# First scale and shift by products with c, the spreading of c moved between the transposes of x, half of x scaled before its transposes

## The chip, the cores and the metric

The kernel runs on one core of a Trainium2 chip, without exchange with other cores. The metric is device time in microseconds of the execution, the median of several runs.

## The reference

One decoder layer on x (256 tokens, 1024 channels). What the change touches is its beginning; three token mixers and a gated merge follow and stay as they are:

```python
shift, scale, gate = jnp.split(c @ w_ada[l] + b_ada[l], 3, axis=-1)
h = rmsnorm(x, norm_pre[l]) * (1.0 + scale[:, None]) + shift[:, None]
proj = h @ w_in[l] + b_in[l]
...
x = x + gate[:, None] * rmsnorm(out, norm_post[l])
```

## The kernel before

The large matrix products are made in fp32 by three reduced-precision (fp32r) products: each weight matrix is split by ScalarE (`w_hi`, a cast) and VectorE (`w_lo`, weight minus cast), the activations likewise (`h_hi`, `h_lo`), and TensorE adds hi by hi, lo by hi and hi by lo in PSUM. In this text PE is TensorE, ACT ScalarE, DVE VectorE, SP SyncE.

**Start.** `heat(n)` issues n full fp32 products of ones (a full fp32 product is two passes in the trace). c lies as 8 columns in `p_sb`; eight full products with an identity spread it over all partitions into `ps_cb`, and DVE copies that into `cb`. x (tokens on partitions) is transposed by 16 `flip`s into four PSUM banks `ptr[0..3]`, named `ps_x`; `x_norm` computes the row factors `r`, and two products spread them along the free axis (`ps_rx`, then `rrow`). `evac_x(i)` reads bank i, multiplies it with `rrow` and writes two of the eight 128-channel blocks of `xn`.

**First wave.** A loop over k, the eight channel blocks, with the names of the code: `a_raw` gets the scale and the shift rows of w_ada for block k, `w_raw` 2048 columns of w_in. `ada_dot` multiplies such rows with `cb` and sums along the row on DVE (into `adac`), which gives scale and shift of the block as columns `acol` and `bcol`. ACT makes `h_hi` and `h_f` from `xn`, DVE `h_lo`. PE then does the 48 products of pass k into eight PSUM banks `w0_0` to `w0_7`, all that there are (the trace calls them `w`): first group 0 to 3 with `hi[0]`, `lo[0]`, then 4 to 7 with `hi[1]`, `lo[1]`, in each half 8 hi by hi and 16 others. The next stage begins with `ps_f`.

**What sets the order.** Each engine does its instructions as the code issues them; the helper class Loom (line 174 in the profile stands for all of its instructions, 204 for its loads) keeps modelled times by which later, woven work is placed, and adds no waits. Tiles come from rings: 4 raw buffers, 3 of `hi`, 3 of `lo`, and PSUM banks of three kinds, `BANKS = dict(mm=3, sd=3, ml=2)`. A new tile in a used buffer waits for the last reader of the old tile. `ptr` takes kinds mm, sd, ml, ml; `ps_cb` two of sd; `w0_0` to `w0_2` are mm, `w0_3` to `w0_5` sd, `w0_6` and `w0_7` ml.

Of the kernel before, what the change touches and what calls it, by code (L numbers as in the profile page):

```python
# [60 lines left out]
CATCH = 7  # L61
BRANCHES = ((2, "c"), (0, "a"), (1, "b"))
AHEAD = {2: ((0, 1), ()), 0: ((0,), (1,)), 1: ((0, 1), ())}
HEAT = (5, 3, 6)
# [212 lines left out]
def trunk(ctx: ExitStack, tc, xtok, wada, wave0, wgrp, wmisc, w1, wbr, wout, par, vbias, out):  # L277
# [26 lines left out]
    def bank(name, kind="mm"):  # L304
        return loom.alloc(psum.tile([128, 512], F32, name=name, tag=kind, bufs=BANKS[kind]), kind, BANKS[kind])
# [39 lines left out]
    ps_cb = [bank("ps_cb", "sd") for _ in range(2)]  # L345
    for i in range(2):
        for j in range(4):
            mm(ps_cb[i][:, 128 * j:128 * j + 128], pc("c", 4 * i + j).broadcast_to([128, 128]), ident, True, True)
        dve.tensor_copy(cb[:, 512 * i:512 * i + 512], ps_cb[i])
        drop(ps_cb[i])  # L350
# [122 lines left out]

    for t in range(2):
        act.activation(xnf[:, D * t:D * t + D], x_sb[:, t], AF.Square, accum_out=ss[:, t:t + 1])
        for k in range(KT):
            flip(ptr[k // 2][:, 256 * (k % 2) + 128 * t:256 * (k % 2) + 128 * t + 128],
                 x_sb[:, t, 128 * k:128 * k + 128])
    act.activation(r, ss, AF.Sqrt, bias=eps, scale=1.0 / D)
    heat(HEAT[1])  # L480

    def x_norm():
# [22 lines left out]
    banks = [bank(f"w0_{f}", kinds[f]) for f in range(8)]  # L505
    for k in range(KT):
        raw = rawt([128, 2, D], "a_raw")
        wraw = rawt([128, 2, 1024], "w_raw")
        for i in range(2):
            loom.load(nc.sync, raw[:, i], wada[k, :, i])  # L510
        for i in range(2):
            loom.load(nc.sync, wraw[:, i], wave0[k, :, 1024 * i:1024 * i + 1024])
        if k == 0:
            dve.tensor_scalar(v, ss, 1.0 / D, 1e-6, op0=OP.mult, op1=OP.add)
        ada_dot(raw[:, 0], 8 + k)
        if k == 0:
            x_norm()
        ada_dot(raw[:, 1], k)
        if k == 0:
            evac_x(0)  # L520
        a, b = acol[:, k:k + 1], bcol[:, k:k + 1]
        dve.scalar_tensor_tensor(a, adac[:, 8 + k:9 + k], 1.0, pc("b_ada", 8 + k), op0=OP.add, op1=OP.add)
        dve.tensor_tensor(b, adac[:, k:k + 1], pc("b_ada", k), op=OP.add)
        dve.tensor_tensor(a, a, pc("npre", k), op=OP.mult)
# [3 lines left out]
        act.copy(hi[0], wraw[:, 0])  # L528
        if 4 < k < CATCH:
            act.copy(hi[1], wraw[:, 1])  # L530
        if k == 0:
            heat(HEAT[2])
        act.activation(h_hi[:, k], xn[:, k], AF.Identity, scale=a, bias=b)
        act.activation(h, xn[:, k], AF.Identity, scale=a, bias=b)
        if k < 5 or k >= CATCH:
            act.copy(hi[1], wraw[:, 1])
        if k == KT - 3:
            act.activation(warm, warm, AF.Sigmoid)
        dve.tensor_tensor(lo[0], wraw[:, 0], hi[0], op=OP.subtract)
# [953 lines left out]
```

## Time and profile before

| | us |
|---|---|
| median of 3 runs (lowest, highest) | 506.78 (506.33, 507.31) |
| the profiled execution's own time | 506.12 |
| its span, first to last instruction | 504.4 |
| PE busy | 492.6 |
| DVE busy | 433.6 |
| ACT busy | 306.5 |

The span lies inside the execution's time; 1.7 us are around it. An engine's busy time tells how near it is to being the bound; what a change is worth is read from the stage that it touches.

### The profile page before, as it was taken

Reading aid. Unit: us, or ns where it says so; the run is one execution under the profiler, and the core shown is the slowest. Engines: PE = TensorE matmul, PEld = TensorE weight load, DVE = VectorE, ACT = ScalarE, POOL = GpSimd, SP = SyncE. Lnnn points to the kernel's source line nnn. Section 1 sums busy time; section 2 is a strip of 40 time slices with the busy share of each in tenths; the row PEclk is TensorE's granted clock in tenths of the full one; section 3 lists DMA queues with packets and bytes.
Section 4 is the critical chain, followed back from the end, with each engine's and each line's share of the span. In section 5 each row is a group of like instructions: output and inputs, shape, how many; then the busy total and the mean of one; then the engine's idle time right before and its main releaser. Section 6 shows DMA issues by size and latency. Waiting matters only on the chain.

```text
span 504.4 us, 8492 instructions
## 1 busy us (share of the span) xinstructions
PE 492.6 (98%) x3229; PEld 437.5 (87%) x3229; DVE 433.6 (86%) x872; ACT 306.5 (61%) x518; POOL 7.3 (1%) x41
## 2 busy tenths in 40 slices
PE   7999999999999999999999999999999999999994
PEld 7999999789878989978899799997888788888883
DVE  3999889999999999999799899669998986756755
ACT  3647665335464759979587874666666835354442
POOL 5000000000000000000000000000000000000000
PEclk9999999999999999999999999999999999999998
DMA  8999964874776243414235236455277586655402
GB/s 308 343 357 340 417 265 176 325 279 164 266 303 252 92 159 97 165 73 168 84 136 199 84 120 251 175 182 210 109 294 299 204 343 233 259 203 209 168 0 83
DMA packets 18200, 105.85 MB, mean 210 GB/s; under 512 B 2152, under 2 KB 2288, under 8 KB 8048
## 3 DMA queue, kind: packets, MB, share of 16 engines
q1 hardware_dynamic: 18016, 105.29, 55.9%
q8 instruction: 25, 0.41, 0.3%
q14 instruction: 15, 0.12, 0.1%
q10 hardware_dynamic: 144, 0.03, 0.0%
HBM read 104.26 MB, written 1.05 MB: 209 GB/s over the span
## 4 chain that ended last, share of the span: by engine, by line
PE 90%; DVE 6%; ACT 2%; issue 1%; DMA 1%; DVEq 0%; ACTq 0%
PE ps_f L174 37%; PE ps_t L174 30%; PE w L174 5%; PE ps_out L174 4%; PE ps_o L174 3%; PE ps_s L174 2%; DVE w_lo L174 2%; DVE a_raw L174 2%; PE ps_c L174 2%; PE ps_p L174 1%; PE ps_qk L174 1%; PE ps_n L174 1%; DMA p_sb<-in_par_dram 1%; ACT w_hi L174 1%; PE ps_cb L174 1%
## 5 line engine op out<-in xcount | busy, mean ns | idle before, releaser
L174 DVE TENSOR_TENSOR w_lo<-w_raw,w_hi 128x1024 fp32r<-128x1024 f32 x148 | 179.8, 1219 | 38.5 <-ACT w_hi L174 37.1
L174 ACT CAST w_hi<-w_raw 128x1024 fp32r<-128x1024 f32 x148 | 154.6, 1045 | 74.7 <-PE ps_t L174 52.4
L174 PE MATMUL ps_f<-h_hi,w_hi 128*128 128x256 f32 x512 | 130.0, 290 | 0.0
L174 PE MATMUL ps_f<-h_lo,w_hi 128*128 128x256 f32 x512 | 126.2, 283 | 0.0
L174 PEld LDWEIGHTS ps_f<-h_hi,w_hi 128*128 128x128 f32 x512 | 98.0, 191 | 1.9 <-issue 1.1
L174 PEld LDWEIGHTS ps_f<-h_lo,w_hi 128*128 128x128 f32 x512 | 98.1, 192 | 0.6 <-issue 0.2
L174 DVE SCALAR_TENSOR_TENSOR acc<-u,p_sb,acc 128x226 f32<-128x226 f32 (+28 forms) x232 | 93.0, 459 | 2.0 <-ACT acc L174 1.9
L174 PE MATMUL ps_f<-h_hi,w_lo 128*128 128x256 f32 x512 | 75.8, 288 | 0.0
L174 PEld LDWEIGHTS ps_f<-h_hi,w_lo 128*128 128x128 f32 x512 | 66.9, 191 | 3.0 <-issue 1.8
L174 PE MATMUL ps_t<-w_hi,h_hi 128*128 128x512 f32 x144 | 57.4, 398 | 0.2 <-DVE gs L174 0.2
L174 PE MATMUL ps_t<-w_hi,h_lo 128*128 128x512 f32 x144 | 56.2, 391 | 0.0
L174 PE MATMUL ps_t<-w_lo,h_hi 128*128 128x512 f32 x144 | 44.9, 393 | 0.0
L174 PEld LDWEIGHTS ps_t<-w_hi,h_hi 128*128 128x128 f32 x144 | 27.1, 188 | 6.8 <-issue 0.8
L174 PEld LDWEIGHTS ps_t<-w_lo,h_hi 128*128 128x128 f32 x144 | 27.0, 188 | 5.7
L174 ACT ACT_TABLE_LOAD x24 | 30.8, 1283 | 1.6 <-PEq L1485 1.2
L174 PEld LDWEIGHTS ps_t<-w_hi,h_lo 128*128 128x128 f32 x144 | 27.1, 188 | 5.3
L174 PE MATMUL w<-h_lo,w_hi 128*128 128x256 f32 x128 | 31.4, 283 | 0.0
L174 PE MATMUL w<-h_hi,w_lo 128*128 128x256 f32 x128 | 31.3, 282 | 0.0
L174 DVE SCALAR_TENSOR_TENSOR a_raw<-a_raw,cb 128x1024 f32<-128x1024 f32 x24 | 28.6, 1218 | 0.0
L174 PEld LDWEIGHTS w<-h_hi,w_lo 128*128 128x128 f32 x128 | 24.5, 191 | 0.0
L174 PEld LDWEIGHTS w<-h_lo,w_hi 128*128 128x128 f32 x128 | 24.5, 191 | 0.0
L174 ACT ACTIVATE pm<-pm,mx 128x16 f32<-128x16 f32 (+2 forms) x48 | 19.0, 401 | 1.9 <-DVE mx L174 1.9
(261 smaller groups left out, 697.7 us busy)
## 6 DMA issues: line engine op xcount, KB each, us to landing
w_raw<-in_wgrp_dram SPq DMA_DIRECT2D x50, 1024.0 KB, 4.9
w_raw<-in_wbr_dram SPq DMA_DIRECT2D x12, 1024.0 KB, 4.8
a_raw<-in_wada_dram SPq DMA_DIRECT2D x16, 512.0 KB, 6.8
w_raw<-in_wave_dram SPq DMA_DIRECT2D x16, 512.0 KB, 6.5
w_raw<-in_w_dram SPq DMA_DIRECT2D x8, 1024.0 KB, 4.8
a_raw<-in_wada_dram SPq DMA_DIRECT2D x4, 1024.0 KB, 4.8
w_raw<-in_wout_dram SPq DMA_DIRECT2D x4, 1024.0 KB, 4.7
vb_mg<-in_vbias_dram SPq DMA_DIRECT2D x3, 512.0 KB, 5.7
```

What stands on the lines that cost most here:

```text
L174: inst = self.pin(fn(*args, **kw))
```

## The change

Scale and shift of block 0 no longer come from `ada_dot`: w_ada's first pair is laid out untransposed, and 16 full products (8 for scale, 8 for shift) with 128x128 pieces of it as stationary operand and c, repeated over 32 columns, as moving operand leave them as columns in PSUM (`ps_a`). The eight products that spread c move between the transposes of x, four behind each half's first four transposes; DVE copies the first half of `cb`, ACT the second, later. Channels 512 to 1023 of x are scaled by `r` in place before they are transposed, so that ACT's evacuation of `ptr[2]` and `ptr[3]` needs only a factor, and two later products with `rrow` on DVE go. The first two `w_raw` come in three loads. In passes 0 and 1 DVE makes `h_hi`, the cast of `hi[0]` goes in two halves, and in pass 0 `lo[0]` does too. Block 1's scale product moves ahead of the last split of pass 0; `evac_x(1)` moves from pass 0 to the end of pass 1. The heats are 8 and 1, before 5, 3 and 6.

```diff
--- before.py
+++ after.py
@@ -59,9 +59,10 @@
 NEARLY = 56
 
 CATCH = 7
+NREP = 32
 BRANCHES = ((2, "c"), (0, "a"), (1, "b"))
-HEAT = (5, 3, 6)
+HEAT = (8, 1)
 LEAD = 2
 BANKS = dict(mm=3, sd=3, ml=2)
@@ -342,12 +343,6 @@
     ident = const.tile([128, 128], F32, name="ident")
     make_identity(nc, ident)
     cb = const.tile([128, D], F32, name="cb")
-    ps_cb = [bank("ps_cb", "sd") for _ in range(2)]
-    for i in range(2):
-        for j in range(4):
-            mm(ps_cb[i][:, 128 * j:128 * j + 128], pc("c", 4 * i + j).broadcast_to([128, 128]), ident, True, True)
-        dve.tensor_copy(cb[:, 512 * i:512 * i + 512], ps_cb[i])
-        drop(ps_cb[i])
@@ -471,13 +466,18 @@
                           rrow[:, None, :].broadcast_to([128, 2, S]), op=OP.mult)
         drop(ptr[i])
 
+    ps_cb = [bank("ps_cb", "sd") for _ in range(2)]
+
+    def flip_x(k, t):
+        flip(ptr[k // 2][:, 256 * (k % 2) + 128 * t:256 * (k % 2) + 128 * t + 128], x_sb[:, t, 128 * k:128 * k + 128])
+
     for t in range(2):
         act.activation(xnf[:, D * t:D * t + D], x_sb[:, t], AF.Square, accum_out=ss[:, t:t + 1])
-        for k in range(KT):
-            flip(ptr[k // 2][:, 256 * (k % 2) + 128 * t:256 * (k % 2) + 128 * t + 128],
-                 x_sb[:, t, 128 * k:128 * k + 128])
+        for k in range(KT // 2):
+            flip_x(k, t)
+        for j in range(4):
+            mm(ps_cb[t][:, 128 * j:128 * j + 128], pc("c", 4 * t + j).broadcast_to([128, 128]), ident, True, True)
     act.activation(r, ss, AF.Sqrt, bias=eps, scale=1.0 / D)
-    heat(HEAT[1])
 
     def x_norm():
         dve.reciprocal(r, r)
@@ -487,6 +487,9 @@
         ps = bank("ps_rx")
         for t in range(2):
             mm(ps[:, 128 * t:128 * t + 128], r[:, t:t + 1].broadcast_to([128, 128]), ident, True, True)
+        late = [x_sb[:, t, D // 2:] for t in range(2)]
+        dve.tensor_scalar(late[0], late[0], r[:, 0:1], None, op0=OP.mult)
+        act.mul(late[1], late[1], r[:, 1:2])
         act.mul(rrow, ps[:, 0:S], -0.5)
         drop(ps)
 
@@ -502,52 +505,87 @@
     bcol = const.tile([128, 8], F32, name="bcol")
 
     kinds = [k for k in BANKS for _ in range(BANKS[k])]
-    banks = [bank(f"w0_{f}", kinds[f]) for f in range(8)]
+    raws_, wraws = [], []
     for k in range(KT):
-        raw = rawt([128, 2, D], "a_raw")
-        wraw = rawt([128, 2, 1024], "w_raw")
-        for i in range(2):
-            loom.load(nc.sync, raw[:, i], wada[k, :, i])
-        for i in range(2):
-            loom.load(nc.sync, wraw[:, i], wave0[k, :, 1024 * i:1024 * i + 1024])
-        if k == 0:
-            dve.tensor_scalar(v, ss, 1.0 / D, 1e-6, op0=OP.mult, op1=OP.add)
-        ada_dot(raw[:, 0], 8 + k)
-        if k == 0:
-            x_norm()
-        ada_dot(raw[:, 1], k)
-        if k == 0:
-            evac_x(0)
-        a, b = acol[:, k:k + 1], bcol[:, k:k + 1]
-        dve.scalar_tensor_tensor(a, adac[:, 8 + k:9 + k], 1.0, pc("b_ada", 8 + k), op0=OP.add, op1=OP.add)
-        dve.tensor_tensor(b, adac[:, k:k + 1], pc("b_ada", k), op=OP.add)
-        dve.tensor_tensor(a, a, pc("npre", k), op=OP.mult)
+        for j in range(k, k + 2 if k == 0 else k + 1 if k > 1 else k):
+            raw = rawt([128, 2, D], "a_raw")
+            wraw = rawt([128, 2, 1024], "w_raw")
+            raws_.append(raw)
+            wraws.append(wraw)
+            for i in range(2):
+                loom.load(nc.sync, raw[:, i], wada[j, :, i])
+            cuts = (0, 512, 1024, 2048) if j < 2 else (0, 1024, 2048)
+            flat = wraw.rearrange("p a b -> p (a b)")
+            for c0, c1 in zip(cuts, cuts[1:]):
+                loom.load(nc.sync, flat[:, c0:c1], wave0[j, :, c0:c1])
+        raw, wraw = raws_[k], wraws[k]
         hi = [ringt(his, [128, 1024], "w_hi", "hi", HIS, F32R) for _ in range(2)]
         lo = [ringt(los, [128, 1024], "w_lo", "lo", LOS, F32R) for _ in range(2)]
         h = h_f[:, k]
-        act.copy(hi[0], wraw[:, 0])
-        if 4 < k < CATCH:
-            act.copy(hi[1], wraw[:, 1])
+        a, b = acol[:, k:k + 1], bcol[:, k:k + 1]
         if k == 0:
-            heat(HEAT[2])
-        act.activation(h_hi[:, k], xn[:, k], AF.Identity, scale=a, bias=b)
+            dve.tensor_copy(cb[:, 0:512], ps_cb[0])
+            drop(ps_cb[0])
+            dve.tensor_scalar(v, ss, 1.0 / D, 1e-6, op0=OP.mult, op1=OP.add)
+            ps_a = [bank("ps_a", kind) for kind in ("mm", "sd")]
+            for i in range(2):
+                for j in range(KT):
+                    mm(ps_a[i][:, 0:NREP], raw[:, i, 128 * j:128 * j + 128], pc("c", j).broadcast_to([128, NREP]),
+                       j == 0, j == KT - 1)
+                if i == 0:
+                    x_norm()
+                    evac_x(0)
+            mods = [p[:, 0:1] for p in ps_a]
+        else:
+            if k > 1:
+                ada_dot(raw[:, 0], 8 + k)
+            ada_dot(raw[:, 1], k)
+            mods = adac[:, 8 + k:9 + k], adac[:, k:k + 1]
+        dve.scalar_tensor_tensor(a, mods[0], 1.0, pc("b_ada", 8 + k), op0=OP.add, op1=OP.add)
+        dve.tensor_tensor(a, a, pc("npre", k), op=OP.mult)
+        dve.tensor_tensor(b, mods[1], pc("b_ada", k), op=OP.add)
+        if k == 0:
+            drop(*ps_a)
+            for t in range(2):
+                for j in range(KT // 2, KT):
+                    flip_x(j, t)
+            heat(HEAT[1])
+        if k < 2:
+            act.copy(hi[0][:, 0:512], wraw[:, 0, 0:512])
+            dve.tensor_scalar(h_hi[:, k], xn[:, k], a, b, op0=OP.mult, op1=OP.add)
+            act.copy(hi[0][:, 512:], wraw[:, 0, 512:])
+        else:
+            act.copy(hi[0], wraw[:, 0])
+            if 4 < k < CATCH:
+                act.copy(hi[1], wraw[:, 1])
+            act.activation(h_hi[:, k], xn[:, k], AF.Identity, scale=a, bias=b)
         act.activation(h, xn[:, k], AF.Identity, scale=a, bias=b)
+        if k == 0:
+            act.copy(cb[:, 512:], ps_cb[1])
+            drop(ps_cb[1])
         if k < 5 or k >= CATCH:
             act.copy(hi[1], wraw[:, 1])
         if k == KT - 3:
             act.activation(warm, warm, AF.Sigmoid)
-        dve.tensor_tensor(lo[0], wraw[:, 0], hi[0], op=OP.subtract)
-        dve.tensor_tensor(h_lo[:, k], h, h_hi[:, k], op=OP.subtract)
         if k == 0:
+            dve.tensor_tensor(lo[0][:, 0:512], wraw[:, 0, 0:512], hi[0][:, 0:512], op=OP.subtract)
+            dve.tensor_tensor(h_lo[:, k], h, h_hi[:, k], op=OP.subtract)
+            dve.tensor_tensor(lo[0][:, 512:], wraw[:, 0, 512:], hi[0][:, 512:], op=OP.subtract)
+            for i in range(2, 4):
+                act.mul(xn[:, 2 * i:2 * i + 2], ptr[i].rearrange("p (k s) -> p k s", k=2), -0.5)
+                drop(ptr[i])
+        else:
+            dve.tensor_tensor(lo[0], wraw[:, 0], hi[0], op=OP.subtract)
+            dve.tensor_tensor(h_lo[:, k], h, h_hi[:, k], op=OP.subtract)
+        if k == 0:
+            ada_dot(raws_[1][:, 0], 9)
+        dve.tensor_tensor(lo[1], wraw[:, 1], hi[1], op=OP.subtract)
+        if k == 1:
             evac_x(1)
-            for i in range(2, 4):
-                act.copy(xn[:, 2 * i:2 * i + 2], ptr[i].rearrange("p (k s) -> p k s", k=2))
-                drop(ptr[i])
-        dve.tensor_tensor(lo[1], wraw[:, 1], hi[1], op=OP.subtract)
-        if k in (3, 5):
-            c = xn[:, k + 1:k + 3]
-            dve.tensor_tensor(c, c, rrow[:, None, :].broadcast_to([128, 2, S]), op=OP.mult)
         drop(raw, wraw)
+
+        if k == 0:
+            banks = [bank(f"w0_{f}", kinds[f]) for f in range(8)]
 
         def w0(f, j, w, x, start, stop):
             c = (f % 4) * 256 + j * 128
...
+    pairs[0] = np.stack([ktiles(wa[i, 0].T) for i in (1, 0)], 1)
```

How the change moves instructions, at three places. The names are those of the tiles with their buffer numbers; a bracket names the engine or DMA queue whose counter the instruction waits for, and a wait for a counter covers all earlier work of that engine.

PE at the program's start, before (`ps_x_157` to `ps_x_160` are `ptr[0]` to `ptr[3]`):

```order
L174 MATMUL ps_heat_94<-ones_84 128x128 [waits Pool_49]
L174 MATMUL ps_heat_94<-ones_84 128x128 x4
L174 MATMUL ps_cb_107<-ident_101,p_sb_90 128x128 [waits DMAHW0_49,Pool_49]
L174 MATMUL ps_cb_107<-ident_101,p_sb_90 128x128 x3
L174 MATMUL ps_cb_108<-ident_101,p_sb_90 128x128 x4
L174 MATMUL ps_x_157<-ident_101,x_sb_89 128x128 [waits DMAHW1_49]
L174 MATMUL ps_x_157<-ident_101,x_sb_89 128x128
L174 MATMUL ps_x_158<-ident_101,x_sb_89 128x128 x2
L174 MATMUL ps_x_159<-ident_101,x_sb_89 128x128 x2
```

And in the change (`ps_x_148` and `ps_x_149` are `ptr[0]` and `ptr[1]`):

```order
L175 MATMUL ps_heat_94<-ones_84 128x128 [waits Pool_49]
L175 MATMUL ps_heat_94<-ones_84 128x128 x7
L175 MATMUL ps_x_148<-ident_104,x_sb_89 128x128 [waits DMAHW1_49,Pool_49]
L175 MATMUL ps_x_148<-ident_104,x_sb_89 128x128
L175 MATMUL ps_x_149<-ident_104,x_sb_89 128x128 x2
L175 MATMUL ps_cb_156<-ident_104,p_sb_90 128x128 [waits DMAHW0_49]
L175 MATMUL ps_cb_156<-ident_104,p_sb_90 128x128 x3
L175 MATMUL ps_x_148<-ident_104,x_sb_89 128x128 [waits DMAHW2_49]
L175 MATMUL ps_x_148<-ident_104,x_sb_89 128x128
L175 MATMUL ps_x_149<-ident_104,x_sb_89 128x128 x2
L175 MATMUL ps_cb_157<-ident_104,p_sb_90 128x128 x4
L175 MATMUL ps_a_203<-p_sb_90,a_raw_183 128x32 [waits DMAHW3_49]
```

The products with c stood ahead of all transposes and now stand behind four of each half; the transposes of `ptr[2]` and `ptr[3]` have moved behind the products `ps_a`.

PE in pass 0, from the end of the first half (groups 0 to 3) into the second, before:

```order
L174 MATMUL w0_3_197<-h_hi_189,w_lo_225 128x256
L174 MATMUL w0_4_198<-h_hi_189,w_hi_224 128x256 [waits Activation_49]
L174 MATMUL w0_4_198<-h_hi_189,w_hi_224 128x256
L174 MATMUL w0_5_199<-h_hi_189,w_hi_224 128x256 [waits DVE_49]
L174 MATMUL w0_5_199<-h_hi_189,w_hi_224 128x256
L174 MATMUL w0_6_200<-h_hi_189,w_hi_224 128x256 [waits Activation_49]
L174 MATMUL w0_6_200<-h_hi_189,w_hi_224 128x256
L174 MATMUL w0_7_201<-h_hi_189,w_hi_224 128x256 [waits Activation_49]
L174 MATMUL w0_7_201<-h_hi_189,w_hi_224 128x256
L174 MATMUL w0_4_198<-h_lo_190,w_hi_224 128x256
L174 MATMUL w0_4_198<-h_hi_189,w_lo_226 128x256 [waits DVE_49]
```

In the change, the same stretch:

```order
L175 MATMUL w0_3_261<-h_hi_178,w_lo_199 128x256
L175 MATMUL w0_4_262<-h_hi_178,w_hi_198 128x256 [waits Activation_49]
L175 MATMUL w0_4_262<-h_hi_178,w_hi_198 128x256
L175 MATMUL w0_5_263<-h_hi_178,w_hi_198 128x256 [waits DVE_49]
L175 MATMUL w0_5_263<-h_hi_178,w_hi_198 128x256
L175 MATMUL w0_6_264<-h_hi_178,w_hi_198 128x256 [waits Activation_49]
L175 MATMUL w0_6_264<-h_hi_178,w_hi_198 128x256
L175 MATMUL w0_7_265<-h_hi_178,w_hi_198 128x256 [waits Activation_49]
L175 MATMUL w0_7_265<-h_hi_178,w_hi_198 128x256
L175 MATMUL w0_4_262<-h_lo_179,w_hi_198 128x256
L175 MATMUL w0_4_262<-h_hi_178,w_lo_200 128x256
```

And the beginning of pass 1 in the change (`w_hi_314`, `w_lo_316` and `h_lo` of block 1):

```order
L175 MATMUL w0_0_258<-h_hi_178,w_hi_314 128x256 [waits Activation_49]
L175 MATMUL w0_0_258<-h_hi_178,w_hi_314 128x256
L175 MATMUL w0_1_259<-h_hi_178,w_hi_314 128x256 x2
L175 MATMUL w0_2_260<-h_hi_178,w_hi_314 128x256 [waits Activation_49]
L175 MATMUL w0_2_260<-h_hi_178,w_hi_314 128x256
L175 MATMUL w0_3_261<-h_hi_178,w_hi_314 128x256 x2
L175 MATMUL w0_0_258<-h_lo_179,w_hi_314 128x256
L175 MATMUL w0_0_258<-h_hi_178,w_lo_316 128x256
```

The first product of group `w0_5` waits for DVE in both. Before, DVE is waited for again for `w_lo_226`, the second split of pass 0; in the change neither `w_lo_200` nor pass 1's `h_lo` and `w_lo_316` has a wait for DVE of its own.

DVE from pass 0's splits on, before (`xn` from `ps_x_158` is `evac_x(1)`; `w_lo_305` and `w_lo_306` are pass 1's):

```order
L174 TENSOR_TENSOR w_lo_225<-w_raw_203,w_hi_223 128x1024 [waits DMAHW5_49,Activation_49]
L174 TENSOR_TENSOR h_lo_190<-h_f_191,h_hi_189 128x256 [waits Activation_49]
L174 TENSOR_TENSOR xn_156<-ps_x_158,rrow_164 128x512 [waits PE_49]
L174 TENSOR_TENSOR w_lo_226<-w_raw_203,w_hi_224 128x1024 [waits DMAHW6_49,Activation_49]
L174 SCALAR_TENSOR_TENSOR a_raw_292,adac_188<-a_raw_292,cb_106 128x1024 [waits DMAHW7_49]
L174 SCALAR_TENSOR_TENSOR a_raw_292,adac_188<-a_raw_292,cb_106 128x1024 [waits DMAHW0_49]
L174 SCALAR_TENSOR_TENSOR acol_192<-adac_188,p_sb_90 128x1 [waits DVE_49]
L174 TENSOR_TENSOR bcol_193<-adac_188,p_sb_90 128x1 [waits DVE_49]
L174 TENSOR_TENSOR acol_192<-acol_192,p_sb_90 128x1 [waits DVE_49]
L174 TENSOR_TENSOR w_lo_305<-w_raw_293,w_hi_303 128x1024 [waits DMAHW1_49,Activation_49]
L174 TENSOR_TENSOR h_lo_190<-h_f_191,h_hi_189 128x256 [waits Activation_49]
L174 TENSOR_TENSOR w_lo_306<-w_raw_293,w_hi_304 128x1024 [waits DMAHW2_49,PE_49,Activation_49]
```

In the change, from the second half of `lo[0]` to `evac_x(1)`, which is `xn` from `ps_x_149`:

```order
L175 TENSOR_TENSOR w_lo_199<-w_raw_184,w_hi_197 128x512 [waits DMAHW6_49]
L175 SCALAR_TENSOR_TENSOR a_raw_190,adac_177<-a_raw_190,cb_109 128x1024 [waits DMAHW0_49,Activation_49]
L175 TENSOR_TENSOR w_lo_200<-w_raw_184,w_hi_198 128x1024 [waits DMAHW7_49,Activation_49]
L175 SCALAR_TENSOR_TENSOR a_raw_190,adac_177<-a_raw_190,cb_109 128x1024 [waits DMAHW1_49]
L175 SCALAR_TENSOR_TENSOR acol_181<-adac_177,p_sb_90 128x1 [waits DVE_49]
L175 TENSOR_TENSOR acol_181<-acol_181,p_sb_90 128x1 [waits DVE_49]
L175 TENSOR_TENSOR bcol_182<-adac_177,p_sb_90 128x1
L175 TENSOR_SCALAR h_hi_178<-xn_147,acol_181,bcol_182 128x256 [waits DVE_49]
L175 TENSOR_TENSOR w_lo_316<-w_raw_191,w_hi_314 128x1024 [waits DMAHW3_49,DMAHW2_49,Activation_49]
L175 TENSOR_TENSOR h_lo_179<-h_f_180,h_hi_178 128x256 [waits DVE_49,Activation_49]
L175 TENSOR_TENSOR w_lo_317<-w_raw_191,w_hi_315 128x1024 [waits DMAHW4_49,PE_49,Activation_49]
L175 TENSOR_TENSOR xn_147<-ps_x_149,rrow_155 128x512
```

`evac_x(1)` stood third and ahead of pass 0's second split; now all DVE work of pass 1 stands ahead of it.

## Rows read from the trace of the kernel before

**Rows 1.** The page: busy time, share and instructions of each engine.

```profile
PE 492.6 (98%) x3229; PEld 437.5 (87%) x3229; DVE 433.6 (86%) x872; ACT 306.5 (61%) x518; POOL 7.3 (1%) x41
```

**Rows 2.** Whom PE waited for, whole span: us in total, times, longest.

```profile
PE w L174 <- ACT h_hi L174: 1.2, 2, 0.8
...
PE ps_t L174 <- DVE w_lo L174: 0.3, 1, 0.3
```

**Rows 3.** PE's timeline to 15 us: start, us; x counts passes; [idle before <-releaser].

```profile
1.05 2.50 PE L174 MATMUL ps_heat<-ones 128*128 128x128 f32 x10 [1.05 <-POOL eps L322]
5.35 3.75 PE L174 MATMUL ps_cb<-ident,p_sb 128*128 128x128 f32 x16 [1.79 <-DMA p_sb<-in_par_dram]
8.89 2.33 PE L174 MATMUL ps_x<-ident,x_sb 128*128 128x128 f32 x16
11.06 0.83 PE L174 MATMUL ps_heat<-ones 128*128 128x128 f32 x6
11.91 0.68 PE L174 MATMUL ps_rx<-ident,xr 128*128 128x128 f32 x4
12.43 1.50 PE L174 MATMUL ps_heat<-ones 128*128 128x128 f32 x12
14.68 1.22 PE L174 MATMUL w<-h_hi,w_hi 128*128 128x256 f32 x8 [0.75 <-ACT h_hi L174]
```

**Rows 4.** PE's timeline in the first wave, and at its end.

```profile
17.65 1.12 PE L174 MATMUL w<-h_hi,w_hi 128*128 128x256 f32 x8
...
56.42 1.12 PE L174 MATMUL w<-h_hi,w_hi 128*128 128x256 f32 x8
...
62.18 0.28 PE L174 MATMUL ps_f<-h_hi,w_hi 128*128 128x256 f32 x1
```

**Rows 5.** DVE's timeline, 11 to 20 us.

```profile
11.01 0.16 DVE L174 RECIPROCAL xr<-xr 128x2 f32<-128x2 f32 x1
...
13.04 0.69 DVE L174 TENSOR_TENSOR xn<-ps_x,rrow 128x512 f32<-128x512 f32 x1
...
15.15 0.42 DVE L174 TENSOR_TENSOR h_lo<-h_f,h_hi 128x256 fp32r<-128x256 f32 x1
15.50 0.68 DVE L174 TENSOR_TENSOR xn<-ps_x,rrow 128x512 f32<-128x512 f32 x1
16.10 1.22 DVE L174 TENSOR_TENSOR w_lo<-w_raw,w_hi 128x1024 fp32r<-128x1024 f32 x1
17.24 1.22 DVE L174 SCALAR_TENSOR_TENSOR a_raw<-a_raw,cb 128x1024 f32<-128x1024 f32 x1
...
19.53 0.15 DVE L174 SCALAR_TENSOR_TENSOR acol<-adac,p_sb 128x1 f32<-128x1 f32 x1
...
19.80 1.22 DVE L174 TENSOR_TENSOR w_lo<-w_raw,w_hi 128x1024 fp32r<-128x1024 f32 x1
```

**Rows 6.** ScalarE's (ACT's) timeline to 13 us.

```profile
5.06 1.06 ACT L174 ACTIVATE xn<-x_sb 128x1024 f32<-128x1024 f32 x1 [2.32 <-DMA x_sb<-in_xtok_dram]
...
12.63 0.38 ACT L174 ACTIVATE rrow<-ps_rx 128x256 f32<-128x256 f32 x1 [4.76 <-PE ps_rx L174]
```

**Rows 7.** PE's timeline at 110 us.

```profile
109.72 0.53 PE L174 MATMUL ps_c<-gather,part 128*128 128x32 f32 x4
110.08 0.36 PE L174 MATMUL ps_f<-h_hi,w_hi 128*128 128x256 f32 x1
```

**Rows 8.** DMA issues from 3 to 6 us: x count, size, median us to landing.

```profile
a_raw<-in_wada_dram SPq DMA_DIRECT2D x2, 512.0 KB, 9.3
```

**Rows 9.** SyncE's timeline from 4 us: its issues.

```profile
4.04 1.51 SPq L204 DMA_DIRECT2D a_raw<-in_wada_dram  x2
```

**Rows 10.** Stretches at the end: length, busy time (x), PEclk, DMA share, GB/s.

```profile
496.00:498.00 2.00, 1.29 (x6) 0.75 (x4) 1.82 (x4) 0.65 (x3) 0.00 (x0) 1.00 0.31 120
498.00:501.00 3.00, 0.00 (x0) 0.00 (x0) 2.72 (x7) 0.28 (x2) 0.00 (x0) 1.00 0.25 95
501.00:502.00 1.00, 0.00 (x0) 0.00 (x0) 0.00 (x0) 0.00 (x0) 0.00 (x0) 0.64 0.88 332
```

## The prediction

> **What bounds the kernel now.** First the page's line of busy shares [rows 1]: TensorE (PE) is busy for 492.6 of 504.4 us, so a microsecond counts only where it starts PE earlier, stops it, or slows it. Then PE's list of waits [rows 2]: after its start it waits 1.2 us for `h_hi` (before the first wave and before one of its later passes) and, as the next longest, 0.3 us once much later. Nothing behind the first wave is slack that could give a late start back. Then PE in order of time [rows 3, 4]: the wave, which is all that the change touches, begins at 14.68 and ends where `ps_f` begins, at 62.18. Its last pass runs from 56.42 to 62.18, 5.76 us for 48 products, 0.12 each, without a wait; eight such passes are 46.1 us and the wave takes 47.5, so its own waits cost 1.4.
>
> **The order, and the place that decides.** The wave needs all eight PSUM banks. Product group `w0_5` gets the bank of `ps_x` number 1 (kind "sd", of which there are three), and may write there only when `evac_x(1)` has read it. Before, that read stands ahead of the wave's first pass on VectorE (DVE): it starts at 15.50 [rows 5], and PE comes to `w0_5` at about 17.9 [rows 4], so the handover costs nothing. In the changed kernel the read comes behind the last split of pass 1. The order shows what PE then waits for: its DVE wait at `w0_5` in pass 0 is the last for a long while, and not even pass 1's first uses of `w_lo` and `h_lo` wait for DVE, so the wait at `w0_5` already covers DVE work of pass 1. PE does 26 products of pass 0, then stops until DVE has done nearly all of pass 1. That wait has no cover: the other 22 products of pass 0 stand behind it on PE's queue, and everything else behind those.
>
> **When DVE gets there.** I follow the new order with the durations of the old rows.
> PE: eight heats keep it at work from 1.05 to about 4.7; x's first half has landed by 5.06 and c by 5.35 [rows 3, 6]. Four transposes and four products with c at the slow pace take 0.9 and 1.7 us. The pace: `ps_cb` took 3.54 us for 16 passes, 0.22 each; the last heats 0.125 each at most. The 16 transposes from 8.89 to 11.06 are 2.17 us, some 4 at the slow pace and 12 at half of it, so the clock rose at about 9.7, when PE had worked for 4.35 us on end. Those are the two levels, 1.2 and 2.4 GHz. With more heats and 0.3 us of idle time in place of 1.8 I take the rise near 6.3; it may be 9.7 again.
> With the rise at 6.3: products with c done at 7.0, transposes of x's other half 7.45, c again 8.35. Sixteen narrow products (32 columns) are new; the nearest rows [rows 7], 32 columns too and two passes to a product, give 0.36 us for two up to the start of the next work, so at most 0.18 each; I take 1.3 us for eight. The first eight end at 9.65. `ps_rx` follows (r is ready by then: half of `cb` copied in 0.7, as `xn` in [rows 5], then 0.9 from the reciprocal to `ps_rx`). From its start to `rrow` 0.72 and to `xn` 1.13 [rows 3, 5, 6]: `xn` starts at 10.8 and ends at 11.4, as the second eight do. a, b and `h_hi` on DVE (like `h_lo`, 0.35) end at 12.15; the wave starts at 12.5 (eight transposes and a heat behind the second eight) in place of 14.68. That is the gain of the change's first part: 2.2 us.
> DVE then does half a split, `h_lo`, half a split (0.6 + 0.35 + 0.6), and at 13.7 the first row product of pass 1, whose data land at 13.3 (issued at 4.04, 9.3 us under way) [rows 8, 9].
> From there to the end of `evac_x(1)`, all from starts of [rows 5]: row product 1.15, split 1.14, row product 1.15, a and b 0.35, `h_hi` 0.35, split 1.14, `h_lo` 0.35, split 1.14, `evac_x(1)` 0.68: 7.45 us. PE goes on at 21.2. Not before 20.75 (data at 13.3 and no other delay); 22.8 if the clock rises only at 9.7, since then every PE step ahead of `h_hi` is later and the row product starts at 15.35.
>
> **The sum.** At 21.2 there remain 22 products (2.6) and seven passes of 5.76 (40.3), now without the 1.4 us of waits, as DVE and ScalarE are ahead: the wave ends at 64.1, 1.9 later than 62.18 (bounds 1.5 and 3.5).
> To that comes the clock. PE stands still from 15.6 to 21.2, 5.6 us. At the end of the program its last product ended at 497.3 (PE is busy for 1.29 of the stretch from 496), and the granted clock was 1.00 up to 501 and 0.64 on average in the next microsecond [rows 10], as full speed up to 501.3 and half from there would give: it fell after 4.0 us without work. So I expect PE to be at 1.2 GHz when it goes on, and to stay there for about the 4.35 us that it took at the start; at half pace that loses 2.1. Bounds: nothing (it doesn't fall), and 3.2, if it takes as long as all the slow work at the start, heats from 1.05 included (2.3 + 4.35).
> The Trainium skill, page "TensorE: Matmul & The Clock Gate", section "HAM oscillation — how this bites in real kernels", says of bursts with long waits between them that each begins at half clock again. The end of this trace agrees for the fall; a fall in mid-program this trace does not have. By the rule the sum has the 2.1, without it not.
> What else the change does lies in the shadow of that stop: two more issues on SyncE, long ahead of need, 1.2 us of `rrow` products taken from DVE in passes 3 and 5, two half-x scalings, one copy of `cb` on ScalarE. Later work is woven in another order; PE's products are the same, and its longest wait there is the 0.3 [rows 2], so I give that 0.5 either way.
> The sum is +4.0 us. The profiled execution took 506.12, so 510.1; the median of the runs is 506.78, 0.66 above it, so the median should come out at **510.8**.
>
> **Rivals.**
> Late clock (0.15): as above, but the rise at 9.7. For it: the trace has a single rise, and it is at 9.7. Against: PE's heats now reach to x's landing. Then +3.5 + 2.1: 512.4.
> No fall (0.13): the stop is there, the clock stays at 2.4 GHz. For it: the only fall seen is at a program's end. Against: 5.6 us is more than the 4.0 there. Then +1.9: 508.7.
> Faster (0.07): DVE's read of `ps_x` number 1 does not hold PE, because what PE waits for at `w0_5` is an earlier DVE step. Then the wave runs from 12.5 for 46.1 us and ends at 58.6, 3.6 earlier: 503.2. It decides from a resume before 19.3 (62.18 less 42.9), or 17.2 if the clock falls. Against: the chain of 7.45 us can't begin before its data at 13.3, and pass 1 has no DVE waits of its own.
> Nothing changes (0.05): a stop that the earlier start just pays for, a resume at 19.3 and no fall.
> The forecast has the remaining 0.60, on its own 509.6 to 511.8. A measurement of this kernel tells about 0.2%, 1.0 us, from no change: slower 0.88, same 0.05, faster 0.07. The range goes from below no fall (508.7 less 0.4 for the early bound of the resume) to the late clock with some of the longer warm-up: 508.2 to 513.2.
>
> **What would show it.** In the changed profile: PE's `w` with a gap of 5 to 6 us between `w0_4` and `w0_5` of pass 0, ended by DVE's `xn`; before it a wave start near 12.5; slices with a granted clock below 1 at about 20 to 26 us; no `h_hi` waits in the wave afterwards; `ps_f` starting near 66. `ps_cb` followed by transposes at the fast pace shows the early rise. Wrong would be: no gap at `w0_5` (the faster rival), products of `w` at 0.12 us right after the gap (no fall), or a gap that lasts beyond 23 (DVE held by something that I have not seen, such as ScalarE's split of pass 1).

## The result, and the profile after

The changed kernel took **511.0 us** in the median of four runs (510.19 to 512.47), the kernel before 506.68: ratio **1.0092** (95% interval 1.0078 to 1.0105), slower by 0.9%. Four more runs, in the experiments, gave 511.77 against 506.12: 1.0107 (1.0093 to 1.0121). The profiled execution is the slowest of the first four, 512.47 (span 510.7). Line 175 is now the helper's line (174 before, 176 in e5 and e8 below).

The page, busy time of each engine (answers to [rows 1]). PE is busy for 5.4 us more with 22 passes more (3251 in place of 3229, at some 0.12 each 2.6 us): the rest is time at a slower pace.

```profile
PE 498.0 (97%) x3251; PEld 443.6 (87%) x3251; DVE 431.7 (85%) x869; ACT 306.2 (60%) x520; POOL 7.3 (1%) x41
```

Whom PE waited for (answers to [rows 2]): the `h_hi` waits of 1.2 us are gone, and one wait of 2.9 us for DVE's `xn` has come.

```profile
PE w L175 <- DVE xn L175: 2.9, 1, 2.9
PE ps_heat L175 <- POOL eps L323: 1.1, 1, 1.1
PE ps_c L175 <- DMA w_raw<-in_w_dram: 0.6, 1, 0.6
```

PE's timeline to 15 us, then around the stop, then the wave's end (answers to [rows 3, 4]).

```profile
1.05 3.55 PE L175 MATMUL ps_heat<-ones 128*128 128x128 f32 x16 [1.05 <-POOL eps L323]
...
7.73 1.92 PE L175 MATMUL ps_a<-p_sb,a_raw 128*128 128x32 f32 x16
9.48 0.69 PE L175 MATMUL ps_rx<-ident,xr 128*128 128x128 f32 x4
10.01 2.50 PE L175 MATMUL ps_a<-p_sb,a_raw 128*128 128x32 f32 x16
12.32 1.95 PE L175 MATMUL ps_x<-ident,x_sb 128*128 128x128 f32 x8
14.06 0.63 PE L175 MATMUL ps_heat<-ones 128*128 128x128 f32 x2
14.34 2.05 PE L175 MATMUL w<-h_hi,w_hi 128*128 128x256 f32 x8
...
18.85 0.40 PE L175 MATMUL w<-h_hi,w_hi 128*128 128x256 f32 x2
22.15 1.65 PE L175 MATMUL w<-h_hi,w_hi 128*128 128x256 f32 x6 [2.90 <-DVE xn L175]
23.60 0.41 PE L175 MATMUL w<-h_lo,w_hi 128*128 128x256 f32 x1
23.81 0.41 PE L175 MATMUL w<-h_hi,w_lo 128*128 128x256 f32 x1
...
62.06 1.12 PE L175 MATMUL w<-h_hi,w_hi 128*128 128x256 f32 x8
64.94 1.12 PE L175 MATMUL w<-h_hi,w_hi 128*128 128x256 f32 x8
67.82 0.28 PE L175 MATMUL ps_f<-h_hi,w_hi 128*128 128x256 f32 x1
```

The wave starts at 14.34 in place of 14.68 and ends at 67.82 in place of 62.18. After two products of `w0_4` PE stops until 22.15, and behind the stop products start 0.21 apart (23.60, 23.81), where the last pass shows 0.12 (5.76 for 48). From the start of `ps_f` to the end of the span are 442.2 us before (504.4 less 62.18) and 442.9 now (510.7 less 67.82), so all but 0.7 us of the loss lies ahead of `ps_f`. A product is listed with 0.28 us though the next one starts 0.12 later, so a delay of less than about 0.16 us counts as busy time and not as idle time.

DVE ahead of `h_hi`, where it waits for the second eight narrow products (`ps_a`), then from the first row product of pass 1 to the read that PE waits for (answers to [rows 5]): 14.61 to 22.10, without a wait.

```profile
12.54 0.16 DVE L175 TENSOR_TENSOR bcol<-ps_a,p_sb 128x1 f32<-128x1 f32 x1 [0.97 <-PE ps_a L175]
...
14.61 1.22 DVE L175 SCALAR_TENSOR_TENSOR a_raw<-a_raw,cb 128x1024 f32<-128x1024 f32 x1
...
20.28 1.22 DVE L175 TENSOR_TENSOR w_lo<-w_raw,w_hi 128x1024 fp32r<-128x1024 f32 x1
21.42 0.68 DVE L175 TENSOR_TENSOR xn<-ps_x,rrow 128x512 f32<-128x512 f32 x1
```

Stretches of 2 us: length, busy time (number) of PE, its weight loads, DVE, ACT and POOL, then the granted clock PEclk, DMA share, GB/s.

```profile
10.00:12.00 2.00, 2.00 (x17) 2.00 (x15) 0.91 (x3) 1.41 (x3) 0.00 (x0) 0.77 1.03 414
12.00:14.00 2.00, 2.00 (x11) 2.00 (x11) 1.42 (x4) 1.26 (x3) 0.00 (x0) 0.50 1.01 408
...
18.00:20.00 2.00, 1.25 (x11) 1.05 (x9) 1.93 (x8) 1.52 (x2) 0.00 (x0) 1.00 1.04 373
20.00:22.00 2.00, 0.00 (x0) 0.00 (x0) 2.00 (x4) 0.02 (x1) 0.00 (x0) 0.83 1.00 350
22.00:24.00 2.00, 1.85 (x8) 1.85 (x9) 2.00 (x4) 0.00 (x0) 0.00 (x0) 0.50 0.97 311
...
28.00:30.00 2.00, 2.00 (x18) 2.00 (x17) 1.56 (x2) 1.12 (x3) 0.00 (x0) 0.97 1.02 418
```

PE was at half clock, 1.2 GHz, in two stretches: one from the stop to about 28 us, as forecast, and one that was not, in 11 to 18 us, where PE was busy without a break. This earlier one hardly counts: it delays the start of a wave that then stands still for DVE anyway. Below, e5 has it and e8 has not, and their waves end at 65.01 and 64.98.

### The profile page after: what moved, and what is told of

It reads as the page before. It is cut to its first block, busy times and chain, and to the rows that moved or that the text cites. A ratio compares the mean times of both kernels' runs of the same rounds, so it can differ in the third digit from the quotient of the medians.

```text
span 510.7 us, 8544 instructions
## 1 busy us (share of the span) xinstructions
PE 498.0 (97%) x3251; PEld 443.6 (87%) x3251; DVE 431.7 (85%) x869; ACT 306.2 (60%) x520; POOL 7.3 (1%) x41
## 4 chain that ended last, share of the span: by engine, by line
PE 89%; DVE 6%; DMA 2%; issue 1%; ACT 0%; DVEq 0%; ACTq 0%
PE ps_f L175 34%; PE ps_t L175 29%; PE w L175 9%; PE ps_out L175 4%; PE ps_o L175 3%; DVE w_lo L175 2%; PE ps_s L175 2%; PE ps_c L175 2%; PE ps_p L175 1%; DMA w_raw<-in_w_dram 1%; PE ps_qk L175 1%; PE ps_n L175 1%; DMA x_sb<-in_xtok_dram 1%; PE ps_a L175 1%; DVE acc L175 1%
## 5 line engine op out<-in xcount | busy, mean ns | idle before, releaser
L175 DVE TENSOR_TENSOR w_lo<-w_raw,w_hi 128x1024 fp32r<-128x1024 f32 (+1 forms) x149 | 180.0, 1212 | 44.7 <-ACT w_hi L175 43.1
L175 ACT CAST w_hi<-w_raw 128x1024 fp32r<-128x1024 f32 (+1 forms) x150 | 154.8, 1034 | 87.3 <-PE ps_t L175 56.5
L175 PE MATMUL ps_f<-h_hi,w_lo 128*128 128x256 f32 x512 | 76.9, 289 | 0.0
L175 PE MATMUL w<-h_lo,w_hi 128*128 128x256 f32 x128 | 33.5, 295 | 0.0
L175 PE MATMUL w<-h_hi,w_lo 128*128 128x256 f32 x128 | 33.4, 295 | 0.0
L175 PEld LDWEIGHTS w<-h_lo,w_hi 128*128 128x128 f32 x128 | 26.3, 206 | 0.0
L175 PEld LDWEIGHTS w<-h_hi,w_lo 128*128 128x128 f32 x128 | 26.2, 205 | 0.0
L175 DVE SCALAR_TENSOR_TENSOR a_raw<-a_raw,cb 128x1024 f32<-128x1024 f32 x22 | 26.2, 1217 | 0.0
L175 PE MATMUL w<-h_hi,w_hi 128*128 128x256 f32 x128 | 20.3, 305 | 2.9 <-DVE xn L175 2.9
```

What stands on the lines that cost most here:

```text
L175: inst = self.pin(fn(*args, **kw))
```

## The experiments

The theory: the late read `evac_x(1)` stops PE at `w0_5`, the standing still makes the clock fall, and these two are the whole loss; the rest of the change is a gain. Rivals: the stop alone costs, and the clock's fall is not paid for; the new 32-column products and their clock cost; the order of later work costs. From `w0_5` on, the wave needs 22 x 0.12 + 7 x 5.76 = 42.96 us at full pace without waits, so in the table "excess" is `ps_f` less the resume less 42.96: what half pace, and waits, took behind the stop. Times in us; each ratio is against the kernel before, timed on the same chip with it (506.36 for e1 to e5, 506.12 for e6 to e9, 506.38 for e10 and e12). A median is of all runs of a kernel; wave, stop and `ps_f` are of its one profiled run.

| kernel | wave starts | stop | resumes | `ps_f` | excess | median | ratio (95%) |
|---|---|---|---|---|---|---|---|
| changed, first profile | 14.34 | 2.90 | 22.15 | 67.82 | 2.71 | 511.0 | 1.0092 (1.0078, 1.0105) |
| e6 changed, again | 13.72 | 5.41 | 22.49 | 67.79 | 2.34 | 511.77 | 1.0107 (1.0093, 1.0121) |
| e7 128 columns | 13.12 | 5.45 | 21.92 | 66.43 | 1.55 | 511.38 | 1.0100 (1.0086, 1.0114) |
| e8 128 columns, stop filled | 13.13 | 0.53, filled | 21.92 | 64.98 | 0.10 | 509.63 | 1.0069 (1.0055, 1.0082) |
| e5 as changed, stop filled in part | 14.14 | 1.56, part filled | 21.95 | 65.01 | 0.10 | 510.11 | 1.0078 (1.0061, 1.0094) |
| e12 read in mid pass 1, 128 | 13.18 | 2.06 | 18.59 | 63.14 | 1.59 | 507.19 | 1.0015 (1.0006, 1.0024) |
| e9 read at end of pass 0, 128 | 12.94 | 0.92 | 17.21 | 60.27 | 0.10 | 504.60 | 0.9968 (0.9955, 0.9980) |
| e10 as e9, 32 columns | 12.99 | 0.88 | 17.22 | 60.28 | 0.10 | 504.90 | 0.9971 (0.9960, 0.9982) |
| e1 read early | 12.83 | none | | 60.47 | | 505.81 | 0.9991 (0.9980, 1.0003) |
| e3 read early, 128 | 12.83 | none | | 61.62 | | 505.34 | 0.9981 (0.9971, 0.9990) |
| e2 before, late read | 15.00 | 5.80 | 24.18 | 68.90 | 1.76 | 512.46 | 1.0120 (1.0107, 1.0133) |

**e1, the read moved back.**

```diff
             dve.tensor_tensor(lo[0][:, 512:], wraw[:, 0, 512:], hi[0][:, 512:], op=OP.subtract)
+            evac_x(1)
...
-        if k == 1:
-            evac_x(1)
```

> The changed kernel with evac_x(1) moved from the end of pass 1 to pass 0, behind the last half split of the first w_lo; nothing else differs, and PE's order is the same. Theory (the stop at w0_5 costs both the stop and a second stretch at 1.2 GHz): the gap of 2.9 us before w0_5 is gone and with it the half pace from 22.1 to 28.1 us (some 3 us), the early half pace at 11 to 18 us stays; ps_f starts near 62.0 in place of 67.8, and the median is 506.0 to 507.0, as the kernel before. Rival 1 (the stop costs only itself, the clock would fall anyway around 21 us): 508 to 509. Rival 2 (the loss lies behind the wave, in the order of later work): ps_f starts near 62 but the median stays at 509 or above.

505.81, a little below the range and not told apart from before. The loss is gone with the one moved step, while PE's order is the changed kernel's; so neither the order of later work nor the products with c as such make it. In the profiled run, the fastest of 12 (504.51), `ps_f` came at 60.47, earlier than I said, since the half pace at 11 to 18 us did not come.

**e2, the late read alone, in the kernel before.**

```diff
         if k == 0:
-            evac_x(1)
             for i in range(2, 4):
...
+        if k == 1:
+            evac_x(1)
         if k in (3, 5):
```

> The kernel before with one edit of the change alone: evac_x(1) at the end of pass 1 in place of pass 0; no narrow products, no new loads, PE's order the same. Theory (the late read is the loss): PE stops at w0_5 from about 17.9 to 22.6 us, then goes on at half pace for some 6 us; ps_f starts near 65.5 without the clock's fall and near 68.5 with it; median 512 to 513.5 with it, 509.5 to 510.5 without. Rival (the narrow products and their clock are the loss, the late read alone is harmless): 506.5 to 507.3.

512.46, in the theory's range: this edit alone makes the kernel before 6.1 us slower, more than the whole change does. PE's row shows the stop; it lasts until 24.18, not 22.6, as DVE also waited twice for 0.5 us for ScalarE's `w_hi` on its way to the read.

```profile
24.18 1.22 PE L174 MATMUL w<-h_hi,w_hi 128*128 128x256 f32 x4 [5.80 <-DVE xn L174]
```

**e3, e1 with 128 columns.**

```diff
-NREP = 32
+NREP = 128
```

> As e1_read_early, and NREP is 128 in place of 32: the 16 products ps_a take c 128 columns wide; the orders of all engines are the same as in e1_read_early. In the profile of the changed kernel a pass of 32 columns takes as long (0.12 us) as one of 128. Theory (the 32 columns are what let the clock fall at 11.06 while PE was busy): no stretch at 1.2 GHz between 5 and 500 us; the wave starts near 12.8 and ps_f near 58.9; median 503 to 504. Rival 1 (the clock falls at 11 us for another reason, as the short waits around it): same half pace, and the time of e1_read_early, 506 to 507. Rival 2 (wide passes are slower after all): the two groups ps_a take over 2.5 us each, and the median is at or above that of e1_read_early.

505.34: better than before by 0.2%, but not 503 to 504, and in no rival's range. The clock held and the wave started at 12.83, as expected; but without a stop its passes did not run in 5.76 us: it took 48.79 us for 46.1 (in e1's profile 47.64). The wave as one stretch, in e3 and then in e9 (below), has PE busy for 48.00 and 46.41 us with the same products; in e3 more of them start late by less than shows as idle time:

```profile
12.83:61.62 48.79, 48.00 (x387) 46.58 (x386) 43.34 (x81) 28.56 (x40) 0.00 (x0) 1.00 1.00 372
```

```profile
12.94:60.27 47.33, 46.41 (x388) 46.21 (x386) 43.25 (x80) 28.60 (x40) 0.00 (x0) 1.00 1.00 379
```

PE's timeline in e3's wave: the `h_hi` waits of [rows 2] are back, and one on `h_lo`.

```profile
20.50 0.38 PE L175 MATMUL w<-h_lo,w_hi 128*128 128x256 f32 x1 [0.19 <-DVE h_lo L175]
43.76 1.22 PE L175 MATMUL w<-h_hi,w_hi 128*128 128x256 f32 x8 [0.20 <-ACT h_hi L175]
50.01 1.22 PE L175 MATMUL w<-h_hi,w_hi 128*128 128x256 f32 x8 [0.24 <-ACT h_hi L175]
```

**e5, the stop filled with work, too little of it.**

```diff
             for f in fs:
+                if k == 0 and f == 5:
+                    for _ in range(FILL):
+                        loom.pin(nc.tensor.matmul(banks[7][:, 0:128], ones, ones, start=True, stop=True))
```

> The changed kernel with 12 products of ones (128 columns, 2.6 us in all at full pace) between w0_4 and w0_5 of pass 0, in the PSUM bank of w0_7, which has been read by then; they wait for nothing that is late, so PE works through most of its stop. The stop itself stays: w0_5 cannot start before 22.15. Theory (standing still is what makes the clock fall at 21.3): no half pace after 22 us, the 24 products and more behind the stop run at 0.12 us; ps_f starts near 65 in place of 67.8; median 507.5 to 508.5. Rival (the clock falls at 21.3 for another reason, or the stretch of half pace is not paid for): 510.5 to 511.5.

510.11, ratio 1.0078 (1.0061 to 1.0094): a miss, in neither range and nearer to the rival's. In the profiled run, which had a half-pace stretch around 12 us again, the half pace behind the stop was gone (resume at 21.95, `ps_f` at 65.01, excess 0.10); yet it took 510.30, no less than the others. Their mean granted clocks are lower (0.988 to 0.994, 0.995 in this one), but a mean does not tell where in a run the clock fell: it also counts the half clock behind the program's last product (in the first profile PEclk is 0.75 in 505 to 507 us, with PE idle). A run whose wave starts near 13 stops for over 5 us, twice what 12 products fill; that this is the reason is not shown, and e8 repeats the test with more products.

**e6, the changed kernel again.**

> The changed kernel, not edited: a second profile and more times of it. In its first four runs the mean granted clock was 0.982 once (the profiled one, with a first fall at 11 us while PE was at work and a second in the stop) and 0.988 to 0.991 three times. Theory (the early fall is chance, and a run without it is the case that the prediction worked out): where the mean clock is 0.988 or more the wave starts at 12.8, PE stops at w0_5 for 5 us up to 20.8 to 21.4 and then works at half pace for 5 to 7 us, ps_f at 66.5 to 67.5, own time 510 to 511; with 0.982 it looks like the first profile, 512 to 513. Rival (the early fall comes every time, in a form that the mean does not show): wave at 14.3 and a gap of 2.9 again.

511.77, above the 510 to 511 that I gave, at mean clocks of 0.988 to 0.991. In this profile the clock does not fall before the stop, and the gap is the forecast's:

```profile
22.49 1.65 PE L175 MATMUL w<-h_hi,w_hi 128*128 128x256 f32 x6 [5.41 <-DVE xn L175]
```

`ps_f` is at 67.79, later than I said, since PE went on at 22.49 and not by 21.4. In part that is a late rise of the pace: the first four passes of `ps_x` took 0.88 (5.03 to 5.91), the next four 0.44 (7.40 to 7.84), so it doubled between them, in the first products with c.

```profile
5.03 1.09 PE L175 MATMUL ps_x<-ident,x_sb 128*128 128x128 f32 x4 [0.19 <-DMA x_sb<-in_xtok_dram]
5.91 1.66 PE L175 MATMUL ps_cb<-ident,p_sb 128*128 128x128 f32 x8
7.40 0.60 PE L175 MATMUL ps_x<-ident,x_sb 128*128 128x128 f32 x4
7.84 1.06 PE L175 MATMUL ps_cb<-ident,p_sb 128*128 128x128 f32 x8
```

**e7 and e8, 128 columns; then the stop filled with 22 products.** Edits as in e3 and e5, FILL = 22.

> The changed kernel with NREP 128 in place of 32; all orders the same. evac_x(1) stays at the end of pass 1. Theory (a product of c 32 columns wide is what now and then lets the clock fall at 11 us, and with the late read the earlier start is only a longer stop): no fall before the stop in any run, wave at 12.8, gap before w0_5 of about 5 us, fall in it; mean clock 0.988 to 0.991 in all runs; median 510 to 511, about the same as the changed kernel, without its slowest runs. Rival (the width has nothing to do with the clock): some runs at a mean clock of 0.982 to 0.985, spread as in the changed kernel.

> As e7_after_wide, with 22 products of ones (128 columns, 0.214 us each at full pace, 4.7 us in all) between w0_4 and w0_5 of pass 0, in the bank of w0_7; 12 of them in e5_fill_stop were too few for a run in which the wave starts at 12.8. The stop stays as long as it was, but PE isn't idle in it. Theory (the idle time makes the clock fall, and the fall is 2 to 3.4 us of the loss): mean clock 0.996, ps_f near 64.1, median 507.0 to 508.2, so 2 to 3.5 less than e7_after_wide. Rival (the stop alone is the loss, or products of ones don't keep the clock): within 0.7 of e7_after_wide.

e7 511.38, e8 509.63, each above its theory's range (510 to 511, 507.0 to 508.2), and e8 below its rival's. The pair has the same orders but for the products of ones, the same wave start and, to 0.01 us, the same resume. PE after the resume in e7, then in e8:

```profile
21.92 1.65 PE L175 MATMUL w<-h_hi,w_hi 128*128 128x256 f32 x6 [5.45 <-DVE xn L175]
...
66.43 0.28 PE L175 MATMUL ps_f<-h_hi,w_hi 128*128 128x256 f32 x1
```

```profile
16.32 5.07 PE L599 MATMUL w<-ones 128*128 128x128 f32 x44
...
21.92 0.98 PE L176 MATMUL w<-h_hi,w_hi 128*128 128x256 f32 x6 [0.53 <-DVE xn L176]
...
64.98 0.28 PE L176 MATMUL ps_f<-h_hi,w_hi 128*128 128x256 f32 x1
```

The granted clock behind the resume, e7 and then e8:

```profile
22.00:24.00 2.00, 2.00 (x9) 2.00 (x10) 2.00 (x3) 0.00 (x0) 0.00 (x0) 0.50 0.99 340
```

```profile
22.00:24.00 2.00, 2.00 (x17) 2.00 (x18) 2.00 (x3) 0.00 (x0) 0.00 (x0) 1.00 0.96 324
```

Six products take 0.98 at full clock and 1.65 at half. The clock's share is 1.45 us at `ps_f` and 1.75 in the median, less than the 2 to 3.5 that I had said, but well outside the 0.7 of the rival by which the stop alone costs. The remaining 3.5 us above the kernel before are the stop itself, less what the rest of the change gains. One run of e7 in four had a mean clock of 0.994 and none was as low as 0.982, but the width is not settled by that.

**e9 and e10, the read one pass sooner: at the end of pass 0.** In e9 NREP is 128, in e10 32.

```diff
-        if k == 1:
+        if k == 0:
             evac_x(1)
```

> As e7_after_wide, with evac_x(1) at the end of pass 0 in place of pass 1: on VectorE behind the first row product and the second split, so that PE, which reaches w0_5 at about 16.0, should stop there for about 1 us, up to 17.0. Theory (a short stop lets VectorE and ScalarE run ahead and takes the place of waits that come later in the wave, and the clock holds): time as e3_early_wide, 505.0 to 505.9. Rival (each microsecond of the stop is paid in full): 506.2 to 506.6.

> The changed kernel with only evac_x(1) moved, to the end of pass 0: e9_read_between with NREP 32 again. Theory (place of the read decides; the width of the products matters only where the clock falls at 11 us, which is some runs at most): median 504.3 to 505.3, and if a run has a mean clock at 0.994 or less it is slower than the others. Rival (most of what e9_read_between gained came from the width): 505.8 to 506.8.

504.60, below the ranges of theory and rival, and 504.90, in the theory's: 0.3% faster than the kernel before, and both beat the changed kernel by over 6 us. DVE reads the bank at 16.47, PE stops for 0.92 us, and that is the wave's only wait: each half pass behind it starts 2.88 after the one before.

```profile
17.21 0.98 PE L175 MATMUL w<-h_hi,w_hi 128*128 128x256 f32 x6 [0.92 <-DVE xn L175]
19.95 1.12 PE L175 MATMUL w<-h_hi,w_hi 128*128 128x256 f32 x8
22.83 1.12 PE L175 MATMUL w<-h_hi,w_hi 128*128 128x256 f32 x8
```

So a microsecond of stop was free, against the rival: the kernels without a stop, e1 and e3, are no faster (the ratios' intervals overlap). That it is free because DVE and ScalarE get ahead in it is argued, not shown by a run of its own; the rows agree (no wait in the wave behind the stop, in any kernel with one, while e1 and e3 have such waits). The width changed nothing here. One thing expected of e10 missed: its three runs at mean clocks of 0.993 and 0.994 took 504.83 to 504.97, no more than the other four (504.65 to 505.04), so a mean clock that low need not cost time.

**e12, one step later than e9's place.**

```diff
             ada_dot(raw[:, 1], k)
+            if k == 1:
+                evac_x(1)
...
-        if k == 1:
-            evac_x(1)
```

> As e9_read_between (128 columns), with evac_x(1) one step later on VectorE, behind the second row product of pass 1 (before a and b of pass 1): PE should stop at w0_5 from 16.1 to about 18.2, 2.1 us in place of 0.9. Theory (a stop is free only as far as it takes the place of waits that come later in the wave, about 1.5 us, and the clock holds through 2.1 us): passes of 5.76 us behind it without waits, ps_f near 61.4, median 505.4 to 506.1, so 1.0 to 1.4 above e9_read_between. Rival 1 (the clock falls in a stop of 2.1 us already): 507 or more and a mean clock of 0.994 or less. Rival 2 (the lead that VectorE wins makes up for 2 us too): 504.3 to 505.0.

507.19: rival 1, as to the median. In the profiled run a stop of 2.06 us was enough for the clock to fall. In six of the 11 runs the mean clock was 0.991 or 0.992, lower than in any run of e9, e10 or the kernel before; the other five, at 0.994 and 0.995, are not told apart by it, and the fastest of them (505.65) is in the theory's range. The stretches show the fall in 19 to 20 us, when PE had been back at work since 18.59:

```profile
18.59 1.06 PE L175 MATMUL w<-h_hi,w_hi 128*128 128x256 f32 x6 [2.06 <-DVE xn L175]
```

```profile
18.00:19.00 1.00, 0.41 (x3) 0.41 (x4) 0.93 (x5) 0.10 (x1) 0.00 (x0) 1.00 0.94 369
19.00:20.00 1.00, 1.00 (x8) 1.00 (x8) 1.00 (x2) 1.00 (x2) 0.00 (x0) 0.67 0.97 352
20.00:21.00 1.00, 1.00 (x7) 1.00 (x7) 1.00 (x3) 0.45 (x1) 0.00 (x0) 0.50 0.96 377
...
23.00:24.00 1.00, 1.00 (x10) 1.00 (x10) 1.00 (x3) 1.00 (x1) 0.00 (x0) 1.00 0.99 360
```

Between e9 and e12 lies one DVE step. At `ps_f` it makes 2.87 us: 1.14 of longer stop, 1.49 of half pace and 0.24 of a later wave start; the ratios differ by 0.47%, 2.4 us.

## Why the prediction was right

**What bounds the kernel** held: with a stop there is no slack behind it, and the 1.4 us of the wave's own waits went, as the sum took it (from 33.26 on every pass takes 5.76).

**The place that decides** held in every profile with the read in pass 1: PE stops after two products of `w0_4`, and DVE's `xn` ends it. e1 and e2 show it from both sides. With e6 to e10 on one scale, the change comes apart: 504.9 (e10) is the change with the read at the end of pass 0, 1.5 us gained (which of its edits brings this was not tested); the longer stop adds about 5.0 (e8 less e9), the clock 1.75 (e7 less e8). That makes 511.7, and e6 measured 511.77.

**When DVE gets there**: the chain was taken as 7.45 us and measured 7.49. Its beginning was mis-sized: 14.61 in place of 13.7, so PE went on at 22.15 in place of 21.2, inside the bounds of 20.75 and 22.8. The term that was too small above all is the narrow products: 1.3 us for eight in the sum, 1.75 measured (7.73 to 9.48), 0.22 each where [rows 7] was read as at most 0.18. DVE waits for the second eight ahead of `h_hi`, 0.97 us here and 0.42 in e7, whose clock did not fall before the stop and whose chain begins at 14.37. The wave's start was taken at 12.5; without disturbance it is 12.8 to 13.2. With the late rise of the pace (e6) it is 13.72, and in the first profile 14.34, by a fall of the clock during the second `ps_a` (16 passes in 2.50 us, 1.92 for the first 16) that no rival had. That start made the gap 2.9 us in place of 5 to 6; e6 has 5.41.

**The sum**: the wave's end without clock was forecast 1.9 us later than before; e8, the same stop with the clock held, has 64.98, 2.8 later. The clock's 2.1 measured 1.55 (e7), 2.34 (e6) and 2.71 (first profile) as excess behind the stop, all within its bounds (of which the upper, half of 2.3 + 4.35, is 3.3 and not 3.2). Together the forecast was +4.0 where the two profiles of the changed kernel have +5.6 at `ps_f`; the median of its first four runs is +4.3, of the second four +5.6. So 510.8 was low, by the late beginning of DVE's chain above all (0.95) and by the clock. That the first median, 511.0, is only 0.2 away is in part luck: the second four runs are 1.0 above the forecast, and at `ps_f` the sum was 1.6 short.

**The reason for the fall of the clock** was right in kind and wrong in its measure: the 4.0 us without work ahead of the fall at the program's end [rows 10] was the yardstick. In the stop the fall came after 2.1 us (first profile: last product ended at 19.25, PEclk 0.83 in 20 to 22 means half from 21.3), and in e12 a stop of 2.06 us was enough. By the 4.0 the clock would have held through the first profile's 2.9 us; that the stop was to be 5.6 hid the error. The Trainium skill, page "TensorE: Matmul & The Clock Gate", section "HAM oscillation — how this bites in real kernels", says that a burst behind a long wait begins at half clock; the products behind 22.15 at 0.21 us agree.

The rise at 9.7, from which the prediction took the length of the half pace, rests on the pace alone: `ps_cb` at 0.22 a pass before and 0.11 in the change. The granted clock of the kernel before is 1.00 in that stretch too:

```profile
6.00:7.00 1.00, 1.00 (x7) 1.00 (x7) 0.00 (x0) 0.88 (x3) 1.00 (x4) 1.00 0.97 356
```

So no row shows 1.2 GHz at the start, and the column cannot be relied on there. Behind the stop column and pace agree.

**Late clock** came in part (e6), **faster** and **nothing changes** did not. What the faster rival needed, a read that does not hold PE for long, is e9: it gives 504.6, 1.5 us faster than before, where that rival's 503.2 would have been 3.6.

## What to carry to other kernels

A step that hands a buffer to the bounding engine may be moved by a few instructions only: here the same 0.68 us read is free at the end of pass 0, costs some 2.4 us one step later and 6.8 at the end of pass 1, since on top of the wait comes half pace behind it. When an early start is bought, look for the next thing that the bounding engine will reach earlier too; the stop, not the saved work, decided this change. A short stop can be worth having where the feeding engines are just behind; measure it, and look at the granted clock behind it.

## What the runs showed of the hardware

- The clock can fall while PE is busy without a break: in the first profile (PE busy 2.00 of 2.00 in 10 to 12 us, PEclk 0.77) and in e5 (2.00 of 2.00, PEclk 0.80), both during products of 32 columns. It did so in two of the five profiles with 32 columns (the changed kernel twice, e1, e5, e10) and in none of the five with 128 (e3, e7, e8, e9, e12). That the width does it is not settled.
- In stops of nearly the same length the clock fell at different times: 2.0 us after PE's last product in e7 (PEclk 0.61 in 18 to 20 us, last product ended at 16.47) and 3.8 in e6 (0.71 in 20 to 22, ended at 17.08). In e12 it fell after PE was back at work. At the program's end it was 4.0 us before, but 2.4 in the first profile (last product ended at 503.58, PEclk 0.75 in 505 to 507).
- A full product of 32 columns saves next to nothing over one of 128: from the first 16 passes of `ps_a` to `ps_rx` 1.75 us with 32, 1.85 with 128 (e3).
